# Square sums of attention heads' outputs: squares as float32 weights against one column of ones

## The chip, the cores and the metric

The kernel runs on one core of one Trainium2 chip, as one launch. The metric is device time in microseconds (us) of that core. Three runs of the kernel before took 1516.12, 1515.57 and 1514.3 us; their median is 1515.57 us.

## The reference, cut to what matters

One encoder layer: RMSNorm, a combined projection, a pooling branch and a differential-attention branch, gates, an output projection, and an MLP. The part that the change touches is the normalisation of each head's output in the attention branch:

```python
def head_rmsnorm(x, g):
    xf = x.astype(jnp.float32)
    return xf * lax.rsqrt(jnp.mean(xf * xf, axis=-1, keepdims=True) + EPS) * g.astype(jnp.float32)

    o = o.transpose(1, 0, 2, 3, 4).reshape(B, S, N_HEADS, V_HEAD_DIM)
    o = head_rmsnorm(o, g_sub) * (1.0 - lambda_init)
```

There are 8 heads, 1024 positions, and 128 values a head and position (`V_HEAD_DIM`). For each head and position the sum of 128 squares is needed.

## The kernel before, in words

All large products run on TensorE in "fp32r" pieces: an operand is split in a high and a low part (`split`, L135 on ACT makes the high part, L136 on DVE or POOL the low one), and `mm3` (L142 to L144) makes three matmuls of them. The kernel has an attention stage, a stage that combines the branches, and the MLP. The attention stage works in groups, one for each pair of head h and block t of 128 positions (64 groups). In each group one token of every kind of work is set down, each for a group some places back: A the projection z for a block (`stage_qkv`), B and C the norms and transposes of q and k, D the scores and softmax (`stage_scores`, L783 to L803), E the transposes of the attention weights (`stage_aT`, L839), F the product with V (`stage_pv`), H the square sums (`stage_ssq`), R the finished norm of a whole head (`stage_norm`, L886). F and H run for every second block, so for 4 pairs p of blocks in each of 8 heads: 32 times each. Beside these, "fillers" set down the projections of the gates (tiles g) and of the pooling branch (tiles u, yp), one unit every second group. A scheduler then sets the order of the instructions on each engine from the kernel's data dependencies, this order of tokens and its own estimate of the times. Each engine runs its list strictly in that order.

What happens to one pair of blocks: `stage_pv` accumulates the head's output, transposed (128 values by 256 positions), in columns 0 to 255 of the PSUM tile `po`. ACT squares it into the SBUF tile `oq` (L863), copies it to `oS` (L864), and the copy goes to DRAM (L865). Then `split` (L869) makes the tile `oqs` of the squares' high part (ACT, L135) and low part (DVE, L136). In `stage_ssq` a 128 by 128 matrix of ones is the weight operand, and the high and low parts stream past it (L876, L877, 256 columns each): columns 256 to 511 of `po` get the sums over the 128 partitions, the same in every row. DVE multiplies each 128 by 128 half with the identity and adds up along the rows (L879, a multiply-and-reduce, followed by a read of its accumulator), so that position q's sum lands in row q of one column of `SS`. Once a head has all 8 columns of `SS`, `stage_norm` works out the factor r (L890 to L895), transposes it on TensorE (L897, tile `trr`), copies it to `rT` on ACT (L899) and stores it (L900); `y_pair` loads it back for the output of the heads (tiles yr, yb, later `by`).

The tile `po` has a single buffer, and so have `oq` and `oqs`. The matrix `ones` is of type fp32r; `f(ones)` reads the same bytes as float32. A matmul whose operands are float32 or fp32r loads its own weights: a trace shows the load as a row of the engine PEld and the product as a row of PE. The transposes (L739, L839, L897) are matmuls in transpose mode, with the float32 data as weights and the identity `identf` streaming past.

Of the kernel before, what the change touches and what calls it, by code (L numbers as in the profile page):

```python
# [9 lines left out]
F32R = mybir.dt.float32r  # L10
I32 = mybir.dt.int32
AF = mybir.ActivationFunctionType
ALU = mybir.AluOpType
# [4 lines left out]
P = 128  # L18
# [49 lines left out]
def encoder_kernel(  # L68
# [21 lines left out]
    nc = tc.nc  # L90
    x, out = x[0], out[0]
# [20 lines left out]
    def pad(pool_, n):  # L112
        pool_.tile([P, n], F32, tag=f"pad{n}", name=f"pad{n}")
# [16 lines left out]
    def f(ap):  # L130
        return ap.bitcast(F32)

    def split(hi, lo, src, lo_eng=None):

        made = nc.scalar.copy(hi, src)  # L135
        (lo_eng or nc.vector).tensor_tensor(lo, src, f(hi), op=ALU.subtract)  # L136
        return made

    def mm3(ps, lhs_hi, lhs_lo, rhs_hi, rhs_lo, first, last, more=False):

        kw = {"skip_group_check": True} if more else {}
        nc.tensor.matmul(ps, lhs_hi, rhs_hi, start=first, stop=False, **kw)  # L142
        nc.tensor.matmul(ps, lhs_hi, rhs_lo, start=False, stop=False, **kw)  # L143
        return nc.tensor.matmul(ps, lhs_lo, rhs_hi, start=False, stop=last, **kw)  # L144
# [62 lines left out]
    identf = const.tile([P, P], F32, name="identf")  # L207
    make_identity(nc, identf)
    ones = const.tile([P, P], F32R, name="ones")
# [211 lines left out]
    with ExitStack() as ph:  # L421
# [5 lines left out]
        def s1(shape, dt, name, tag, bufs=1):  # L427
            return sp.tile(shape, dt, tag=tag, name=name, bufs=bufs)
# [249 lines left out]
        st = {}  # L678
        ATs = {}
        Zs = {}  # L680
        SS = {}
# [167 lines left out]
        def stage_pv(h, p):  # L849
            V, views = KV[h][1], ATs.pop((h, p))[0]  # L850
            po = ps_o.tile([P, 512], F32, tag="o", name=f"po{h}_{p}")
            nkt = 2 * p + 2
            for kt in range(nkt):
                v = V[kt // 4]
                mm3(
                    po[:, 0:256], v[:, kt % 4, 0, :], v[:, kt % 4, 1, :],
                    views[kt][0], views[kt][1], kt == 0, kt == nkt - 1,
                )
                if kt % 2 and kt < nkt - 1:
                    yield  # L860
            oS = s1([P, 256], F32, f"oS{h}_{p}", "oS", 2)
            oq = s1([P, 256], F32, f"oq{h}_{p}", "oq")
            nc.scalar.activation(oq, po[:, 0:256], AF.Square)  # L863
            nc.scalar.copy(oS, po[:, 0:256])  # L864
            nc.scalar.dma_start(y_dram[h * P : (h + 1) * P, p * 256 : (p + 1) * 256], oS)  # L865
            if not (h or p):
                pad(sp, 16)
            oqs = s1([P, 2, 256], F32R, f"oqs{h}_{p}", "oqs")
            split(oqs[:, 0, :], oqs[:, 1, :], oq)  # L869
            st[h, p, "o"] = (po, oq, oqs)  # L870
            yield

        def stage_ssq(h, p):

            po, oq, oqs = st.pop((h, p, "o"))
            nc.tensor.matmul(po[:, 256:512], ones, oqs[:, 0, :], start=True, stop=False)  # L876
            nc.tensor.matmul(po[:, 256:512], ones, oqs[:, 1, :], start=False, stop=True)  # L877
            for i in range(2):
                nc.vector.tensor_tensor_reduce(  # L879
                    out=oq[:, i * P : (i + 1) * P], in0=po[:, 256 + i * P : 256 + (i + 1) * P], in1=identf,  # L880
                    scale=1.0, scalar=0.0, op0=ALU.mult, op1=ALU.add,
                    accum_out=SS[h][:, 2 * p + i : 2 * p + i + 1],
                )
            yield

        def stage_norm(h):  # L886
# [21 lines left out]
        def stage(w, g):  # L908
            h, t = divmod(g, NT)
            if w == "A":  # L910
                if t == 0:
                    head_start(h)
                yield from stage_qkv(h, t)
            elif w == "B":
                yield from stage_prep(h, t)
            elif w == "C" and t % 2:
                yield from stage_qkT(h, t - 1)
            elif w == "D":
                yield from stage_scores(h, t)
            elif w == "E":  # L920
                yield from stage_aT(h, t)
            elif w == "F" and t % 2:
                yield from stage_pv(h, t // 2)
            elif w == "H" and t % 2:
                yield from stage_ssq(h, t // 2)
            elif w == "R" and t == NT - 1:
                yield from stage_norm(h)
            elif w == "W" and t == 0 and h:
                for kp in range(NK // 2):
                    load_w(h, kp)  # L930
                    split_w(h, kp, nc.gpsimd)
# [61 lines left out]
        for g in range(-2, N + 10):  # L993
# [33 lines left out]
            for tok in ORDER:  # L1027
                if tok not in gens:
                    i = g - tok[1]
# [767 lines left out]
```

## Time and profile before

| | |
|---|---|
| median of three runs | 1515.57 us |
| the profiled execution's own time | 1515.89 us |
| its span, first to last instruction | 1514.1 us |
| PE (matmuls) busy | 1506.0 us, 7590 instructions |
| PEld (weight loads) busy | 1308.1 us, 7590 instructions |
| DVE busy | 1062.3 us |
| ACT busy | 809.3 us |
| POOL busy | 352.5 us |
| granted TensorE clock | 1.00 throughout |

The profile is of one execution. PE's rows show when a matmul starts and a modelled end: successive matmuls overlap, so the busy time of a row is longer than what it adds. What a matmul adds to PE's time is read from the distance between one start and the next. In a timeline the columns are the start, the duration, the engine, the line and operation, the tiles (written<-read), the shapes and a count; in square brackets stands how long the engine sat idle before it, and what ended that.

### The profile page before, as it was taken

The numbers are of one execution on the slowest core, as the hardware profiler recorded it, in microseconds if no ns is written. First come the engines' busy times: TensorE is split into PE (matmuls) and PEld (weight loads), VectorE is DVE, ScalarE is ACT, GpSimd is POOL, SyncE is SP. The second block draws the span as 40 slices with busy tenths as digits, with TensorE's granted clock in tenths as the row PEclk, the third lists the DMA queues.
The fourth block names the chain that finished last, engine by engine and source line by source line (L and its number), as shares of the span: only waits on it lengthen the run. The fifth ranks groups of instructions, "written<-read, shape, count | busy, mean of one in ns | idle before, by whom it ended". The sixth has DMA issues, their size and how long they took to land.

```text
span 1514.1 us, 22055 instructions
## 1 busy us (share of the span) xinstructions
PE 1506.0 (99%) x7590; PEld 1308.1 (86%) x7590; DVE 1062.3 (70%) x2170; ACT 809.3 (53%) x1671; POOL 352.5 (23%) x457
## 2 busy tenths in 40 slices
PE   9999999999999999999999999999999999999999
PEld 8999998999999989888888888888888888888887
DVE  7776768877888777745469899667656687556662
ACT  6656566655656564653544477556555634333331
POOL 4545644353526453321330000000000000000000
PEclk9999999999999999999999999999999999999999
DMA  7223333422434344437865734454433799437750
GB/s 228 70 85 118 105 97 108 126 87 65 150 117 147 98 129 151 160 117 248 308 216 195 237 132 144 156 187 154 152 125 112 285 361 388 161 125 259 227 189 28
DMA packets 211210, 247.86 MB, mean 164 GB/s; under 512 B 12981, under 2 KB 146074, under 8 KB 211098
## 3 DMA queue, kind: packets, MB, share of 16 engines
q1 hardware_dynamic: 193530, 219.01, 43.7%
q10 hardware_dynamic: 17568, 27.44, 4.9%
q8 instruction: 60, 0.98, 0.3%
q14 instruction: 52, 0.43, 0.1%
HBM read 172.97 MB, written 73.43 MB: 163 GB/s over the span
## 4 chain that ended last, share of the span: by engine, by line
PE 96%; DMA 1%; ACT 1%; DVE 1%; issue 1%; SPq 0%; POOL 0%; DVEq 0%; ACTq 0%; POOLq 0%
PE z L144 5%; PE z L142 5%; PE z L143 5%; PE Da L143 4%; PE Da L142 4%; PE Da L144 4%; PE g L142 4%; PE g L144 4%; PE g L143 4%; PE X L142 3%; PE X L144 3%; PE Db L143 3%; PE Db L142 3%; PE X L143 3%; PE Db L144 3%; PE sc L783 2%
## 5 line engine op out<-in xcount | busy, mean ns | idle before, releaser
L144 PE MATMUL z<-wqkv,hT 128*128 128x384 f32 x512 | 174.0, 340 | 0.0
L142 PE MATMUL z<-wqkv,hT 128*128 128x384 f32 x512 | 173.5, 340 | 0.3 <-ACT hT L445 0.2
L143 PE MATMUL z<-wqkv,hT 128*128 128x384 f32 x512 | 172.9, 338 | 0.0
L794 ACT ACTIVATE s<-s,nm 128x256 f32<-128x256 f32 (+7 forms) x128 | 99.4, 777 | 77.6 <-DVE nm L786 76.8
L716 POOL TENSOR_TENSOR ms<-ms,mhalf 128x4 f32<-128x4 f32 x64 | 71.1, 1110 | 164.4 <-DVE ms L715 162.9
L142 PE MATMUL g<-hT,fwgate 128*128 128x512 f32 x256 | 101.2, 395 | 0.6 <-ACT yps L340 0.4
L144 PE MATMUL g<-hT,fwgate 128*128 128x512 f32 x256 | 100.8, 394 | 0.0
L143 PE MATMUL g<-hT,fwgate 128*128 128x512 f32 x256 | 100.6, 393 | 0.0
L142 PEld LDWEIGHTS z<-wqkv,hT 128*128 128x128 f32 x512 | 96.3, 188 | 3.2 <-ACT hT L445 0.8
L143 PEld LDWEIGHTS z<-wqkv,hT 128*128 128x128 f32 x512 | 96.3, 188 | 2.5 <-DVE wqkv L445 0.3
L144 PEld LDWEIGHTS z<-wqkv,hT 128*128 128x128 f32 x512 | 96.2, 188 | 2.3 <-DVE hT L445 0.5
L786 DVE CUSTOM_DVE_ANT_0 s<-sc,dist 128x512 f32<-128x512 f32 (+3 forms) x128 | 71.8, 567 | 19.4 <-PE sc L784 13.8
L136 DVE TENSOR_TENSOR AS<-s,AS 128x512 fp32r<-128x512 f32 x64 | 43.4, 686 | 33.9 <-ACT AS L135 33.8
L783 PE MATMUL sc<-K,Q 128*128 128x512 f32 (+2 forms) x192 | 66.5, 351 | 0.2 <-DVE nm L786 0.2
L784 PE MATMUL sc<-K,Q 128*128 128x512 f32 (+2 forms) x192 | 65.0, 345 | 0.0
L136 POOL TENSOR_TENSOR wqkv<-rqkv,wqkv 128x384 fp32r<-128x384 f32 x56 | 58.9, 1069 | 23.2 <-ACT wqkv L135 22.9
L136 POOL TENSOR_TENSOR fwgate<-frgate,fwgate 128x512 fp32r<-128x512 f32 x32 | 43.7, 1367 | 58.4 <-ACT fwgate L135 58.3
L142 PEld LDWEIGHTS g<-hT,fwgate 128*128 128x128 f32 x256 | 48.1, 188 | 9.4 <-ACT yps L340 0.7
L144 PEld LDWEIGHTS g<-hT,fwgate 128*128 128x128 f32 x256 | 48.1, 188 | 9.2
L143 PEld LDWEIGHTS g<-hT,fwgate 128*128 128x128 f32 x256 | 48.1, 188 | 8.6
L136 DVE TENSOR_TENSOR AT_0l<-ta,AT_0h 128x512 fp32r<-128x512 f32 (+1 forms) x48 | 31.9, 666 | 30.1 <-ACT AT_0h L135 26.2
L379 POOL TENSOR_TENSOR wd<-wd 128x128 f32<-128x128 f32 (+1 forms) x64 | 50.2, 791 | 8.6 <-ACT wd L981 5.9
(513 smaller groups left out, 4614.6 us busy)
## 6 DMA issues: line engine op xcount, KB each, us to landing
wd<-in_w_down_dram SPq DMA_DIRECT2D x48, 512.0 KB, 5.4
wu<-in_w_up_dram SPq DMA_DIRECT2D x32, 512.0 KB, 4.4
udS<-us SPq DMA_DIRECT2D x64, 256.0 KB, 3.7
ur<-udS SPq DMA_DIRECT2D x32, 512.0 KB, 3.5
rqkv<-in_w_in_dram SPq DMA_DIRECT2D x64, 192.0 KB, 2.8
ur<-ud SPq DMA_DIRECT2D x24, 512.0 KB, 4.5
frgate<-in_w_gate_dram SPq DMA_DIRECT2D x32, 256.0 KB, 2.6
g_dram<-go ACTq DMA_DIRECT2D x32, 256.0 KB, 2.0
```

The lines of the kernel that those rows point to most:

```text
L136: (lo_eng or nc.vector).tensor_tensor(lo, src, f(hi), op=ALU.subtract)
L142: nc.tensor.matmul(ps, lhs_hi, rhs_hi, start=first, stop=False, **kw)
L143: nc.tensor.matmul(ps, lhs_hi, rhs_lo, start=False, stop=False, **kw)
L144: return nc.tensor.matmul(ps, lhs_lo, rhs_hi, start=False, stop=last, **kw)
L379: eng.tensor_tensor(out_, a, b, op=ALU.subtract)
L716: powered[0] = nc.gpsimd.tensor_tensor(ms, ms, mhalf[:, 0:4], op=ALU.pow)
L783: nc.tensor.matmul(dst, Q[:, i, 0, :], rhs, start=True, stop=False)
L784: nc.tensor.matmul(dst, Q[:, i, 1, :], rhs, start=False, stop=True)
L786: nc.vector.tensor_tensor_reduce(out=s[i][:, c : c + w], in0=sc[:, 0:w], in1=dist[:, o0 + c : o0 + c + w], scale=2.0 ** -(h + 1), scalar=B ...
L794: exped[0] = nc.scalar.activation(s[i][:, 0:n], s[i][:, 0:n], AF.Exp, bias=last, scale=-1.0, accum_out=Z[:, i, t : t + 1])
```

## The change

The squares are no longer split in two parts, and the tile `oqs` is gone. In `stage_ssq` the roles are turned: a 128 by 128 half of `oq`, read as float32, is the weight operand, and one column of the ones, read as float32, streams past it. The result is one column of `po` with position q's sum in row q. There are two such matmuls, one for each half, in place of the two fp32r matmuls of 256 columns. ACT copies the two columns to `SS`; the identity, the multiply-and-reduce and the accumulator reads on DVE are gone. The rest of the kernel's text is the same.

```diff
-            oqs = s1([P, 2, 256], F32R, f"oqs{h}_{p}", "oqs")
-            split(oqs[:, 0, :], oqs[:, 1, :], oq)
-            st[h, p, "o"] = (po, oq, oqs)
+            st[h, p, "o"] = (po, oq)
             yield
 
         def stage_ssq(h, p):
 
-            po, oq, oqs = st.pop((h, p, "o"))
-            nc.tensor.matmul(po[:, 256:512], ones, oqs[:, 0, :], start=True, stop=False)
-            nc.tensor.matmul(po[:, 256:512], ones, oqs[:, 1, :], start=False, stop=True)
+            po, oq = st.pop((h, p, "o"))
             for i in range(2):
-                nc.vector.tensor_tensor_reduce(
-                    out=oq[:, i * P : (i + 1) * P], in0=po[:, 256 + i * P : 256 + (i + 1) * P], in1=identf,
-                    scale=1.0, scalar=0.0, op0=ALU.mult, op1=ALU.add,
-                    accum_out=SS[h][:, 2 * p + i : 2 * p + i + 1],
-                )
+                nc.tensor.matmul(po[:, 256 + i : 257 + i], oq[:, i * P : (i + 1) * P], f(ones)[:, 0:1], start=True, stop=True)
+            nc.scalar.copy(SS[h][:, 2 * p : 2 * p + 2], po[:, 256:258])
             yield
```

In the changed kernel the two matmuls are line 875 and the copy is line 876. The scheduler makes the lists anew, so other instructions change places too. Here are two places around the first pair of blocks of the seventh head (h = 6, p = 0). On PE, before; `po_0` is the pair's PSUM tile, z and g are projections, sc scores, trr the transposed factor of the head before:

```order
L142 MATMUL z_0_6889<-wqkv_5_6661,hT_0_0_186 128x384
L897 MATMUL trr_6751<-identf,r_6744 8x128
L876 MATMUL po_0_6766<-oqs_0_6778,ones 128x256
L877 MATMUL po_0_6766<-oqs_0_6778,ones 128x256
L143 MATMUL z_0_6889<-wqkv_5_6661,hT_0_0_186 128x384
L144 MATMUL z_0_6889<-wqkv_5_6661,hT_0_1_187 128x384
L142 MATMUL z_0_6889<-wqkv_6_6667,hT_0_0_188 128x384
L142 MATMUL g_1_6822<-hT_1_0_461,fwgate_0_6571 128x512
```

On PE, in the changed kernel:

```order
L142 MATMUL z_0_6789<-wqkv_2_6553,hT_0_0_184 128x384
L783 MATMUL sc_4_0_0_6771<-K_0_5853,Q_4_6627 128x384
L875 MATMUL po_0_6670<-ones,oq_0_6678 128x1 x2
L784 MATMUL sc_4_0_0_6771<-K_0_5853,Q_4_6627 128x384
L143 MATMUL z_0_6789<-wqkv_2_6553,hT_0_0_184 128x384
L144 MATMUL z_0_6789<-wqkv_2_6553,hT_0_1_185 128x384
L142 MATMUL z_0_6789<-wqkv_3_6556,hT_0_0_184 128x384
L890 MATMUL trr_6655<-identf,r_6648 8x128
```

The two matmuls of a pair stand side by side, and earlier: two of the projection z's eight steps are done there, where five were.

On ACT at the same place, before; K, Q and V are the head's operands, s its scores, wqkv the next head's weights:

```order
L864 COPY oS_0_6773<-po_0_6766 128x256
L135 CAST wqkv_5_6661<-rqkv_2_6655 128x384
L712 ACTIVATE sq<-z_7_6781 128x4x64
L135 CAST V_1_5940<-z_7_6781 128x128
L755 CAST Q_4_6723<-tk_4_6718 64x256
L750 ACTIVATE K_1_5938<-tk_4_6718,ggh_5943 64x256
L135 CAST oqs_0_6778<-oq_0_6774 128x256
L865 DMA y_dram<-oS_0_6773 128x256
L135 CAST wqkv_6_6667<-rqkv_3_6664 128x384
```

On ACT, in the changed kernel, from the last instructions ahead of the new copy:

```order
L752 CAST Q_4_6627<-tk_4_6622 64x256
L135 CAST wqkv_5_6565<-rqkv_2_6559 128x384
L876 COPY SS_5858<-po_0_6670 128x2
L341 DMA p_dram<-yps_1_6720 128x512
L135 CAST wqkv_6_6571<-rqkv_3_6568 128x384
L892 COPY rT_6657<-trr_6655 8x128
L135 CAST wqkv_7_6574<-rqkv_3_6568 128x384
L893 DMA r_dram<-rT_6657 8x128
L755 CAST Q_4_6627<-tk_4_6622 64x256
```

The cast of the squares is gone from the list, and the copy of the sums stands eleven places behind the copy to `oS`; casts of the next head's weights stand behind it.

## Prediction

> **What bounds the kernel now.** I read the page's busy times first, then busy times by stretch, then PE's timeline.
>
> ```profile
> span 1514.1 us, 22055 instructions
> ...
> PE 1506.0 (99%) x7590; PEld 1308.1 (86%) x7590; DVE 1062.3 (70%) x2170; ACT 809.3 (53%) x1671; POOL 352.5 (23%) x457
> ```
>
> PE is busy for 1506.0 of 1514.1 us. The instructions in question run between 70 and 690 us (their rows are below), in the attention stage, so I ask for the busy times of that stretch and of the rest:
>
> ```profile
> 70.00:690.00 620.00, 617.92 (x3560) 567.71 (x3559) 460.26 (x1276) 363.89 (x899) 279.66 (x359) 1.00 0.37 118
> 690.00:1514.00 824.00, 819.84 (x3648) 678.60 (x3646) 551.17 (x757) 398.39 (x651) 41.40 (x34) 1.00 0.58 199
> ```
>
> The columns after the length are PE, PEld, DVE, ACT and POOL, then the granted clock. In the stage PE idles 2.1 of 620 us, at full clock; DVE is free for 160 us and ACT for 256 us. Behind it PE idles 4.2 of 824 us. So a step that PE does more or less moves the end by nearly its own length, and a step of DVE or ACT counts only where PE stands still for it.
>
> PE's rows overlap, so what a matmul adds is read from start to start. This is PE's timeline at one of the 32 places (start, duration, line):
>
> ```profile
> 306.10 0.34 PE L784 MATMUL sc<-K,Q 128*128 128x384 f32 x1
> 306.27 0.28 PE L876 MATMUL po<-oqs,ones 128*128 128x256 f32 x1
> 306.39 0.27 PE L897 MATMUL trr<-identf,r 128*8 128x128 f32 x1
> 306.41 0.42 PE L142 MATMUL z<-wqkv,hT 128*128 128x384 f32 x1
> 306.67 0.28 PE L877 MATMUL po<-oqs,ones 128*128 128x256 f32 x1
> 306.79 0.34 PE L143 MATMUL z<-wqkv,hT 128*128 128x384 f32 x1
> ...
> 307.38 0.34 PE L142 MATMUL z<-wqkv,hT 128*128 128x384 f32 x1
> 307.55 0.49 PE L839 MATMUL ta<-identf,s 128*128 128x128 f32 x3
> 307.80 0.42 PE L143 MATMUL z<-wqkv,hT 128*128 128x384 f32 x1
> 308.06 0.34 PE L144 MATMUL z<-wqkv,hT 128*128 128x384 f32 x1
> 308.23 0.34 PE L142 MATMUL z<-wqkv,hT 128*128 128x384 f32 x1
> ```
>
> Two prices come out. A matmul of the old pair takes 0.12 us of PE (306.27 to 306.39, 306.67 to 306.79), a matmul of 384 columns 0.17 (307.38 to 307.55). The three transposes have float32 weights of 128 by 128: from 307.55 to 308.06 three of them and one z pass, 0.51 us; less 0.17 for the z, 0.34 remain, 0.11 each. They stream 128 columns, half of what the old pair's matmuls do, yet cost nearly as much. So I read 0.11 as the time of a weight load that no long stream covers. The transpose of r shows the same from the other side: it streams 128 columns too, but loads only 8 columns of weights, and the next matmul starts 0.02 us after it.
>
> **The change part by part.** *PE.* Removed: 2 fp32r matmuls in each of 32 places, 2 x 0.12 = 0.24 us a place, 7.7 us in all. Added: 2 matmuls a place with float32 weights of 128 by 128 and a stream of one column. The stream is next to nothing, so the price is that of the loads, and the question is how many there are. The trace of before has no plain float32 matmul. The changed program as built answers it: its list for TensorE holds 7654 weight loads and 7654 matmuls, where the page counts 7590 of each before. 7590 less the 64 removed plus 64 x 2 is 7654: each new matmul is executed as two loads, each with a pass of its own. A place then has four loads instead of two, 4 x 0.11 = 0.44 us by the transposes' price, or 0.20 more than before; 32 x 0.20 = 6.4 us more on PE.
>
> The bounds of that price: below, the two loads of a matmul cost together what a transpose's one does, 2 x 0.11 = 0.22 a place, 0.02 less than before, a gain of 0.6 us. Above, each load also carries two passes of its stream (high and low part of the ones), and each further pass costs a start-to-start of the kind seen at 306.39 (0.02, call it 0.03): 4 x 0.14 = 0.56, 0.32 more, 10.2 us. The rows of the loads themselves (time of all, then mean ns of one) lead to the same upper end:
>
> ```profile
> L143 PEld LDWEIGHTS z<-wqkv,hT 128*128 128x128 f32 x512 | 96.3, 188 | 2.5 <-DVE wqkv L445 0.3
> ...
> L839 PEld LDWEIGHTS ta<-identf,s 128*128 128x128 f32 x288 | 35.7, 140 | 6.5 <-DVE AT L136 1.0 <-ACT V L135 0.8
> ```
>
> Neither is what a load adds, since loads overlap their neighbours: the transposes come 0.11 apart with loads of 0.140. If the new loads did not overlap at all, four of 0.140 would again be 0.56. I take 0.11 a load, since the transposes are the only float32 weights in the trace that stand side by side under short streams, as the new ones do.
>
> The Trainium skill, FP8 and Floating Point Precision, TensorE Precision Notes, says that a true FP32 product takes four passes through the array (high and low part of each operand), and TensorE: Matmul & The Clock Gate, Terms, says that the transpose mode is four times faster for FP32, so that a transpose's price would not be a plain float32 matmul's. No run shown here has a plain float32 matmul; if each of four passes cost a load, the sum would be the last rival's below.
>
> *DVE.* Removed, from the views of the two tiles and of line 879:
>
> ```profile
> L135 ACT CAST oqs<-oq x32: 391/407/425, 75.2 to 680.1; 128x256 fp32r<-128x256 f32 x32
> L136 DVE TENSOR_TENSOR oqs<-oq,oqs x32: 404/426/1231, 76.3 to 680.5; 128x256 fp32r<-128x256 f32 x32
> ```
>
> ```profile
> L879 DVE CUSTOM_DVE_ANT_0 oq<-po,identf x64: 238/285/292, 78.4 to 685.5; 128x128 f32<-128x128 f32 x64
> L879 DVE DVE_READ_ACCUMULATOR2_ANT SS<- x64: 75/83/86, 78.7 to 685.7; 128x1 f32 x64
> its engine sat idle before it (us, times) until:
>   PE po L877: 3.9, 6
> ```
>
> By the medians (ns), 32 x 426 + 64 x 285 + 64 x 83 = 37.2 us of DVE go. It is off PE's path but for the places where PE waits for DVE, and those are few:
>
> ```profile
> 249.62 0.39 PE L142 MATMUL yp<-mix,wgrp 128*128 128x512 f32 x1
> 249.85 0.40 PE L143 MATMUL yp<-mix,wgrp 128*128 128x512 f32 x1
> 250.09 0.40 PE L144 MATMUL yp<-mix,wgrp 128*128 128x512 f32 x1
> 250.86 0.63 PE L839 MATMUL ta<-identf,s 128*128 128x128 f32 x4 [0.38 <-DVE s L803]
> 252.30 0.44 PE L839 MATMUL ta<-identf,s 128*128 128x128 f32 x2 [0.81 <-DVE AT L136]
> 252.90 0.51 PE L783 MATMUL sc<-K,Q 128*128 128x512 f32 x1 [0.17 <-DVE nm L786]
> ```
>
> ```profile
> 542.55 0.36 PE L876 MATMUL po<-oqs,ones 128*128 128x256 f32 x1
> 543.08 0.38 PE L877 MATMUL po<-oqs,ones 128*128 128x256 f32 x1 [0.16 <-DVE oqs L136]
> ...
> 543.64 0.34 PE L142 MATMUL z<-wqkv,hT 128*128 128x384 f32 x1
> 544.37 0.50 PE L142 MATMUL g<-hT,fwgate 128*128 128x512 f32 x1 [0.39 <-ACT yps L340]
> ```
>
> Start to start less the usual price (0.23 for 512 columns, 0.11 a transpose, 0.12, 0.17): 0.54, 1.00, 0.38, 0.41 and 0.56, together 2.9 us. That is all that a lighter DVE and ACT can return here. One of them, the 0.41 at L877, waits for the removed split itself and goes for certain; the others depend on where the new lists put things. I take nothing for them and keep 2.9 us as the lower end.
>
> *ACT.* The cast (407 ns, above) goes, a copy of 128 by 2 comes; the nearest row is the copy of the 8 by 128 factor:
>
> ```profile
> L899 ACT COPY rT<-trr x8: 238/256/257, 152.0 to 694.0; 8x128 f32<-8x128 f32 x8
> ```
>
> ACT wins some 0.15 us a place, 4.8 us in all, under 256 us of free time. But the copy must wait for PE's pair, where the cast waited for ACT's own square. Behind it on ACT stand the casts of the next head's weights and of Q, for which PE waits later. Before, DVE waited for L877 6 times, 3.9 us in all; if ACT waits as long and PE feels half, that is 2 us, and nothing if the list has the copy late, as at the place shown (eleven places behind the copy to oS). Value taken: nothing; upper end 2 us.
>
> *The tail.* The last head's sums feed r, r_dram, the tiles yr and then by, whose products start only here:
>
> ```profile
> L142 PE MATMUL bX<-by,wa x16: 389/389/389, 740.3 to 750.5; 128*128 128x512 f32 x16
> ...
> L135 ACT CAST by<-ry x15: 615/619/624, 706.8 to 751.9; 128x512 fp32r<-128x512 f32 x15
> ```
>
> The first cast ends 33 us ahead of the first product, so the copy's 0.26 us in this chain costs nothing. No DMA is added or moved past another queue by the code itself.
>
> *Sum.* +6.4 us on PE, nothing elsewhere: 1515.89 + 6.4 = 1522.3 for the profiled execution, whose own time lies 0.3 us above the median of the three runs; against the median, 1515.57 + 6.4 = 1522.0. The case's own range: all 2.9 us of waits returned, 1519.1; 0.14 a load, 1525.8.
>
> **The rivals.** (1) *One load's price.* The two loads of a matmul overlap, or the second is so short that a matmul costs 0.11 in all. For it: the only float32 weights in the trace do cost 0.11. Against: they are counted once each, the new ones twice. Result: 0.6 us less, up to 2 us of waits less: 1513 to 1515, no change that can be told (3 us, 0.2%, is about what a measurement of this kernel tells from none).
>
> (2) *Faster, the waits go.* The mechanism is DVE's queue: 37.2 us less in it, and PE finds s, AT and nm ready at 250 and 543 us. With all of the 2.9 us returned, the sum changes its sign where a load adds 0.083 us: 32 x (4 x 0.083 - 0.24) = 2.9. A gain over 3 us needs 0.059 and less, which is the price of (1): 1515.57 - 0.6 - 2.9 = 1512.1. For it: PE's waits in the stage are mostly for DVE. Against: the 0.11, and that the last of the five waits is for ACT.
>
> (3) *The new order stalls.* The lists are made anew on every engine; a wait of PE such as that at 252.30 (1.0 us) may come up at two to five new places, with ACT's copy in front of the casts as the likeliest. 1522.0 + 2 to 5: 1524 to 1527. For it: PE has no slack. Against: DVE and ACT both have less to do.
>
> (4) *Every pass loads.* Four passes a matmul, each at 0.11: 8 x 0.11 = 0.88 a place, 0.64 more, 20.5 us: 1536.1. Against: the built program has two loads a matmul. By the four passes of the Trainium skill's page this is the time, if none of them is hidden.
>
> **How the numbers follow.** The forecast 0.75, (1) 0.12, (2) 0.04, (3) 0.05, (4) 0.04. The likeliest gives 1522.0. The forecast's own 1519.1 to 1525.8 and (3) are in the range; I widen it to 1517 below, for a load slightly under 0.11 with some waits returned, and to 1528 above, for a load of 0.14 together with ACT's 2 us (1527.8). Left out are (1), (2) and (4), 0.20. Slower by over 0.2% are the forecast, (3) and (4), 0.84; within 0.2% is (1), 0.12; faster is (2), 0.04.
>
> **What would show it.** Right: PE and PEld count 7654, line 875 appears 128 times on each; from the start of the first of a group to the next z after it about 0.44 us more than the z alone; DVE's busy time near 1025 us, ACT's near 804.5; idle PE in the attention stage near 2 us; the stage from 70 us to the last L875 about 6 us longer, the rest unchanged. Wrong: starts of line 875 0.05 us apart (1), 64 rows in place of 128, or 0.2 apart (4), or waits on ACT's copy (3).

## The result, and the profile after

The changed kernel takes 1519.37 us (median of 11 runs, 1518.5 to 1519.9), the kernel before 1515.54 us beside it (11 runs, 1514.3 to 1516.12): a ratio of 1.0025, 95% interval 1.0016 to 1.0034. It is 3.8 us slower. Forecast were 6.4 us, 1522.0, in a range from 1517 to 1528. The profiled executions differ by 3.3 us (1515.89 and 1519.16; spans 1514.1 and 1517.3).

The page of the changed kernel, its busy times:

```profile
span 1517.3 us, 22020 instructions
...
PE 1511.0 (100%) x7654; PEld 1314.8 (87%) x7654; DVE 1026.0 (68%) x2010; ACT 801.2 (53%) x1671; POOL 355.0 (23%) x457
```

PE and PEld count 7654, as the built program did; DVE lost 36.3 us, ACT 8.1. Now the busy times of the attention stage (PE, PEld, DVE, ACT, POOL):

```profile
70.00:690.00 620.00, 619.63 (x3611) 571.40 (x3610) 423.68 (x1114) 354.93 (x898) 282.44 (x358) 1.00 0.37 117
```

PE idles 0.4 us of 620 where it idled 2.1. The instructions of the new line on PE, and the copy on ACT, by their lines:

```profile
L875 PEld LDWEIGHTS po<-ones,oq x128: 187/192/225, 77.2 to 686.8; 128*128 128x128 f32 x128
L875 PE MATMUL po<-ones,oq x128: 164/250/250, 77.4 to 686.8; 128*128 128x1 f32 x128
...
  ACT SS L876: 2.3, 4
```

```profile
L876 ACT COPY SS<-po x32: 137/160/172, 78.8 to 687.1; 128x2 f32<-128x2 f32 x32
```

Each of the 64 matmuls is two loads and two passes: 128 rows of each. ACT waited for them 4 times, 2.3 us in all, and its copy took 0.16 us, not the 0.26 of the nearest row. PE's timeline at one of the 32 places shows the price:

```profile
213.77 0.34 PE L143 MATMUL z<-wqkv,hT 128*128 128x384 f32 x1
213.94 0.50 PE L875 MATMUL po<-ones,oq 128*128 128x1 f32 x4
214.31 0.42 PE L144 MATMUL z<-wqkv,hT 128*128 128x384 f32 x1
214.56 0.33 PE L142 MATMUL z<-wqkv,hT 128*128 128x384 f32 x1
```

From 213.94 to 214.56 stand four passes and one z: 0.62 us, less 0.17 for the z, 0.45, or 0.112 a load. Here and below, "a load" in such a price means one weight load with its one short pass: every run here has them in equal number, so only the two together have a price. Over the 32 places that is 32 x (0.45 - 0.24) = 6.7 us more than the old pairs.

What brings 6.7 down to 3.8 is in the same timeline, near the place where PE had waited for s, AT and nm:

```profile
250.05 0.34 PE L144 MATMUL z<-wqkv,hT 128*128 128x384 f32 x1
250.23 0.60 PE L839 MATMUL ta<-identf,s 128*128 128x128 f32 x4
250.58 0.42 PE L142 MATMUL z<-wqkv,hT 128*128 128x384 f32 x1
...
251.37 0.34 PE L143 MATMUL z<-wqkv,hT 128*128 128x384 f32 x1
251.54 0.38 PE L839 MATMUL ta<-identf,s 128*128 128x128 f32 x2
251.68 0.42 PE L144 MATMUL z<-wqkv,hT 128*128 128x384 f32 x1
```

The four and the two transposes stand there without a gap, and z matmuls lie between them. The one longer wait left in the stage is a new one, of 0.5 us:

```profile
383.34 0.33 PE L142 MATMUL z<-wqkv,hT 128*128 128x384 f32 x1
384.04 0.45 PE L143 MATMUL z<-wqkv,hT 128*128 128x384 f32 x1 [0.37 <-POOL wqkv L136]
```

### The profile page after: what moved, and what is told of

It is laid out like the page before. It is cut to its first block, busy times and chain, and to the rows that moved or that the text cites. A ratio compares the mean times of both kernels' runs of the same rounds, so it can differ in the third digit from the quotient of the medians.

```text
span 1517.3 us, 22020 instructions
## 1 busy us (share of the span) xinstructions
PE 1511.0 (100%) x7654; PEld 1314.8 (87%) x7654; DVE 1026.0 (68%) x2010; ACT 801.2 (53%) x1671; POOL 355.0 (23%) x457
## 4 chain that ended last, share of the span: by engine, by line
PE 99%; DVE 1%; ACT 0%; issue 0%; POOL 0%; DVEq 0%; ACTq 0%; POOLq 0%
PE z L144 6%; PE z L143 6%; PE z L142 6%; PE g L143 4%; PE g L144 4%; PE g L142 4%; PE Da L144 4%; PE Da L143 4%; PE Da L142 4%; PE X L142 3%; PE Db L144 3%; PE X L144 3%; PE Db L143 3%; PE X L143 3%; PE Db L142 3%; PE sc L783 2%
```

## The experiments

Theory: the time is the sum of two terms, PE's loads (+6.7 us; the expectations write 6.6) and waits of PE that go because DVE has 37 us less to do. First rival: the waits went because the scheduler made new lists that happened to fall well. Second rival: float32 matmuls of one column have another price than their loads. The first four runs take the change apart.

**TensorE's part as before, DVE's part gone** (against the kernel before):

```diff
-            oq = s1([P, 256], F32, f"oq{h}_{p}", "oq")
+            oq = s1([P, 256], F32R, f"oq{h}_{p}", "oq")
...
-            oqs = s1([P, 2, 256], F32R, f"oqs{h}_{p}", "oqs")
-            split(oqs[:, 0, :], oqs[:, 1, :], oq)
...
-            nc.tensor.matmul(po[:, 256:512], ones, oqs[:, 0, :], start=True, stop=False)
-            nc.tensor.matmul(po[:, 256:512], ones, oqs[:, 1, :], start=False, stop=True)
-            for i in range(2):
-                nc.vector.tensor_tensor_reduce(
...
+            nc.tensor.matmul(po[:, 256:512], ones, oq, start=True, stop=False)
+            nc.tensor.matmul(po[:, 256:512], ones, oq, start=False, stop=True)
+            nc.scalar.copy(SS[h][:, 2 * p : 2 * p + 2], po[:, 256:258])
```

> TensorE's part as before, DVE's part gone: ACT writes the squares as fp32r, both old 256-column matmuls read that one tile, and ACT copies two columns of their result. The low parts and the diagonal are left out, so the sums are not the reference's. Theory (the sum is PE's loads plus PE's waits for DVE that go): PE's work is that of before, and the 2.6 us of waits over 0.15 us that the trace of before has and that of the changed kernel has not are returned by the lighter DVE: 1515.5 - 2.6 = 1512.9 us, 1512 to 1514. Rival (the waits went because the lists were made anew and fell well, not because of DVE's load): a new list falls as it may, 1515.5 and up to 2 us either way, with waits of PE for DVE in the attention stage as before.

Measured: 1514.19 us, ratio 0.9991 (0.9982 to 1.0): 1.3 us less, half of what the theory had, and just outside its range; the interval ends at 1, so the gain is only just told from none. ACT's cast of the squares is gone here too, and its copy is there, as in the changed kernel. The busy times of the stage and the longest of PE's waits in it:

```profile
70.00:690.00 620.00, 618.54 (x3568) 568.73 (x3567) 429.96 (x1116) 355.88 (x900) 281.92 (x359) 1.00 0.37 117
```

```profile
408.48 0.34 PE L143 MATMUL z<-wqkv,hT 128*128 128x384 f32 x1
409.79 0.44 PE L839 MATMUL ta<-identf,s 128*128 128x128 f32 x2 [0.97 <-DVE AT L136]
```

The waits of before are gone, but PE still idles 1.5 us, at a place where it had not waited: DVE's lighter queue is not enough by itself; the list of instructions seems to have a say.

**TensorE's part as changed, DVE's part kept** (against the changed kernel):

```diff
+            oqs = s1([P, 2, 256], F32R, f"oqs{h}_{p}", "oqs")
+            split(oqs[:, 0, :], oqs[:, 1, :], oq)
...
+            idle = s1([P, 2], F32, f"idle{h}_{p}", "idle")
+            for i in range(2):
+                nc.vector.tensor_tensor_reduce(
+                    out=f(oqs[:, i, 0:P]), in0=po[:, 130:258], in1=identf,
+                    scale=1.0, scalar=0.0, op0=ALU.mult, op1=ALU.add,
+                    accum_out=idle[:, i : i + 1],
+                )
```

> TensorE's part as changed, DVE's part kept: the split of the squares on ACT and DVE and the two multiply-and-reduce passes of DVE behind the matmuls stay, their results unused. Theory: the loads cost 32 x (4 x 0.112 - 0.24) = 6.6 us and DVE's waits are back: 1515.5 + 6.6 = 1522.1 us, 1521 to 1523. Rival (the lists): as the changed kernel, 1519.4 us, since DVE's 37 us are under cover.

Measured: 1521.62 us, ratio 1.0041 (1.0028 to 1.0053), as the theory had it: 2.2 us over the changed kernel. With DVE's work back, PE idles 1.4 us in the stage:

```profile
70.00:690.00 620.00, 618.57 (x3600) 569.78 (x3599) 455.29 (x1267) 364.07 (x927) 278.11 (x357) 1.00 0.37 116
```

But the two longest waits in the stage name ACT, not DVE:

```profile
150.07 0.27 PE L899 MATMUL trr<-identf,r 128*8 128x128 f32 x1
150.90 0.50 PE L142 MATMUL g<-hT,fwgate 128*128 128x512 f32 x1 [0.56 <-ACT go L349]
...
628.54 0.49 PE L839 MATMUL ta<-identf,s 128*128 128x128 f32 x3
629.49 0.66 PE L839 MATMUL ta<-identf,s 128*128 128x128 f32 x4 [0.46 <-ACT Q L755]
```

This kernel also has the cast of the squares back on ACT, beside the new copy. So the time fits the theory, but that DVE's queue made these waits is not shown: the cast on ACT or the new list may have.

**One load a matmul** (against the changed kernel):

```diff
-            oq = s1([P, 256], F32, f"oq{h}_{p}", "oq")
+            oq = s1([P, 256], F32R, f"oq{h}_{p}", "oq")
...
-                nc.tensor.matmul(po[:, 256 + i : 257 + i], oq[:, i * P : (i + 1) * P], f(ones)[:, 0:1], start=True, stop=True)
-            nc.scalar.copy(SS[h][:, 2 * p : 2 * p + 2], po[:, 256:258])
+                nc.tensor.matmul(po[:, 256 + 2 * i : 258 + 2 * i], oq[:, i * P : (i + 1) * P], ones[:, 0:2], start=True, stop=True)
+            nc.scalar.copy(SS[h][:, 2 * p : 2 * p + 2], po[:, 256:260:2])
```

> As changed, but ACT rounds the squares to fp32r as it writes them, and they are fp32r weights against two columns of the ones: the low parts of the squares are left out. The built list has 7590 loads, so one load a matmul. Theory (the price is 0.112 us a load): 2 x 0.112 - 0.24 = -0.02 us a place, -0.5 us, and the waits go as in the changed kernel: 1515.5 - 0.5 - 2.6 = 1512.4 us, 1511.5 to 1513.5. Rival (float32 or one-column matmuls have a price of their own beside the load): 0.15 us or more a matmul, 1514 us or more.

Measured: 1512.90 us, ratio 0.9983 (0.9975 to 0.9992). It is faster than both kernels, 6.5 us under the changed one for 64 loads fewer, 0.10 us each. The trace has 64 rows of each kind, and at one place:

```profile
147.24 0.28 PE L875 MATMUL po<-ones,oq 128*128 128x2 f32 x2
147.38 0.43 PE L143 MATMUL z<-wqkv,hT 128*128 128x384 f32 x1
147.64 0.33 PE L144 MATMUL z<-wqkv,hT 128*128 128x384 f32 x1
```

Two passes and a z take 0.40 us, less 0.17, 0.115 a load. The second rival falls: a load with a short pass costs the same in fp32r and in float32, and a plain float32 matmul costs two of them and nothing beside.

**Every float32 matmul twice** (against the changed kernel):

```diff
                 nc.tensor.matmul(po[:, 256 + i : 257 + i], oq[:, i * P : (i + 1) * P], f(ones)[:, 0:1], start=True, stop=True)
+                nc.tensor.matmul(po[:, 258 + i : 259 + i], oq[:, i * P : (i + 1) * P], f(ones)[:, 0:1], start=True, stop=True)
```

> As changed, but each of the two float32 matmuls is made twice, the second time into two columns that nobody reads. Theory: four more loads a place, 32 x 4 x 0.112 = 14.3 us: 1519.4 + 14.3 = 1533.7 us, 1532.5 to 1535. Rival (the four loads run partly under waits of PE that are there anyway): under 1531 us.

Measured: 1532.99 us, ratio 1.0115 (1.0102 to 1.0129): 13.6 us for 128 more loads, 0.106 each. That is 0.7 us less than the theory's 14.3, so at most a twentieth of it was hidden.

The next two runs give the same work other lists, by setting the square sums down one group later:

```diff
-O = "B1 C2 H7 D4 R8 E5 F6 W-2 A0"
+O = "B1 C2 H8 D4 R8 E5 F6 W-2 A0"
```

**The kernel before with H8.**

> The kernel before with its square sums set down one group later (token H8 instead of H7), so the same work in other lists. Theory (the waits follow DVE's load): waits of PE over 0.15 us in the attention stage stay at 2 to 3.5 us, as in the two kernels run so far with DVE's part in place (3.1 and 2.3), and the time at 1515 to 1516.5 us. Rival (the luck of the lists): waits under 1 us and 1513 to 1514 us are as likely.

Measured: 1516.97 us beside 1515.83 for the kernel before, ratio 1.0008 (0.9999 to 1.0017). It came out 0.5 us above the theory's range; no change can be told. PE idles 1.7 us in the stage:

```profile
70.00:690.00 620.00, 618.29 (x3557) 567.16 (x3556) 457.23 (x1274) 365.31 (x899) 278.85 (x359) 1.00 0.37 117
```

**The changed kernel with H8.**

> The changed kernel with token H8 instead of H7. Theory: DVE's load is as light as in the changed kernel, so waits over 0.15 us in the attention stage are 0.5 to 1.8 us, as in the four kernels run so far without DVE's part (0.5 to 1.8), and the time is 1519 to 1521 us. Rival (lists): waits of 2 to 3 us, 1521 to 1522.5 us.

Measured: 1521.79 us, ratio 1.0042 (1.0029 to 1.0054), 2.4 us above the changed kernel and in the rival's range. DVE has no more to do than in the changed kernel, yet PE idles 2.0 us in the stage, and one wait is as long as the worst of before:

```profile
70.00:690.00 620.00, 618.05 (x3597) 569.14 (x3596) 428.39 (x1113) 354.08 (x896) 280.94 (x359) 1.00 0.37 115
```

```profile
412.72 0.33 PE L143 MATMUL z<-wqkv,hT 128*128 128x384 f32 x1
414.19 0.44 PE L839 MATMUL ta<-identf,s 128*128 128x128 f32 x2 [1.13 <-DVE AT L136]
```

So the list alone moves these kernels by up to 2.4 us, as much as the waits in question.

**128 columns of ones instead of one** (against the changed kernel):

```diff
-                nc.tensor.matmul(po[:, 256 + i : 257 + i], oq[:, i * P : (i + 1) * P], f(ones)[:, 0:1], start=True, stop=True)
-            nc.scalar.copy(SS[h][:, 2 * p : 2 * p + 2], po[:, 256:258])
+                nc.tensor.matmul(po[:, 256 + i * P : 256 + (i + 1) * P], oq[:, i * P : (i + 1) * P], f(ones), start=True, stop=True)
+            nc.scalar.copy(SS[h][:, 2 * p : 2 * p + 2], po[:, 256:512:P])
```

> The changed kernel with all 128 columns of the ones streaming past each float32 weight half, instead of one; ACT copies every 128th column. Theory (the load is the price, and a stream up to its length hides under it): a stream of 128 fp32r columns lies under 0.11 us here, and if float32 streams take twice the passes they just fill it: starts 0.11 to 0.12 apart, 1519 to 1521 us. Rival (each pass of a float32 stream adds its own time, another 0.05 us a pass at 128 columns, two a load): 0.16 to 0.21 apart, 32 x 4 x 0.05 to 0.1 = 6 to 13 us more, 1526 to 1532 us.

Measured: 1520.38 us, ratio 1.0031 (1.0019 to 1.0043), 1.0 us above the changed kernel: 128 times the columns for nearly the same time.

```profile
147.43 0.34 PE L142 MATMUL z<-wqkv,hT 128*128 128x384 f32 x1
147.61 0.61 PE L875 MATMUL po<-ones,oq 128*128 128x128 f32 x4
147.97 0.42 PE L783 MATMUL sc<-K,Q 128*128 128x384 f32 x1
148.23 0.34 PE L143 MATMUL z<-wqkv,hT 128*128 128x384 f32 x1
```

From 147.61 to 148.23 again 0.62 us for four passes and a 384-column matmul. The price of a load with its pass stays the same up to 128 columns, so below that it is not the stream that sets it. That it is the load is argued from this, not shown.

Three more runs repeat the first three with H8, to see which term holds in two sets of lists.

**TensorE's part as before, DVE's part gone, H8.**

> TensorE's part as before and DVE's part gone (as in the first experiment, low parts and diagonal left out), with token H8. Theory (three terms that add: loads, DVE's part 1.4 to 2.3 us, the list with H8 1.3 to 2.4 us more): 1517.0 less 1.4 to 2.3: 1514.7 to 1515.6 us. Rival (DVE's part did nothing, the lists did it all): as the kernel before with H8, 1516.5 us or more.

Measured: 1514.41 us, ratio 0.9991 (0.9982 to 1.0); 2.6 us under the kernel before with H8, 0.3 below the theory's range.

**TensorE's part as changed, DVE's part kept, H8.**

> TensorE's part as changed and DVE's part kept (results unused), with token H8. Theory: the changed kernel with H8, 1521.8 us, plus DVE's 1.4 to 2.3: 1523.2 to 1524.1 us. Rival: as the changed kernel with H8, 1521.3 to 1522.3 us.

Measured: 1524.11 us, ratio 1.0051 (1.0038 to 1.0064), at the theory's upper end; but the profile, whose execution took the same 1524.11 us, shows that the time came from elsewhere. In the stage PE idles only 0.2 us. Behind it, it waits for ACT's evacuation of a gate tile (go), and this is what follows:

```profile
706.54 0.39 PE L144 MATMUL bp<-ypT,wbp 128*128 128x512 f32 x1
708.76 0.50 PE L142 MATMUL bp<-ypT,wbp 128*128 128x512 f32 x1 [1.83 <-ACT go L349]
709.10 0.39 PE L143 MATMUL bp<-ypT,wbp 128*128 128x512 f32 x1
...
710.03 0.59 PE L144 MATMUL bp<-ypT,wbp 128*128 128x512 f32 x1
710.42 0.63 PE L142 MATMUL bp<-ypT,wbp 128*128 128x512 f32 x1
...
713.41 0.43 PE L143 MATMUL bp<-ypT,wbp 128*128 128x512 f32 x1
```

On ACT two casts of by stand ahead of that evacuation and wait 8.3 us for a DMA:

```profile
706.99 1.14 ACT L135 CAST by<-ry 128x512 fp32r<-128x512 f32 x2 [8.31 <-DMA ry<-ys]
708.03 0.68 ACT L349 ACTIVATE go<-g,cols 128x512 f32<-128x512 f32 x1
```

The wait costs 2.0 us (2.22 from start to start, less 0.23), and the eight matmuls from 710.03 to 713.41 take 0.42 us each instead of 0.23, 1.5 us more. Without these 3.5 us this execution would be under the changed kernel with H8. The five executions also fall in two groups: three took 1524.1 to 1524.7 us at a mean granted clock of 0.999, two took 1522.1 and 1522.7 us at 1.000, which is what one would see if the slow stretch came in three of them; only one was profiled. So the agreement with the expected number is luck and proves nothing here.

**One load a matmul, H8.**

> One fp32r load a matmul (low parts of the squares left out), with token H8. Theory: 7.1 us of loads (64 of 0.112) under the changed kernel with H8: 1521.8 - 7.1 = 1514.7 us, 1513.7 to 1515.7. Rival (the lists matter more than the loads): 1512.9 us as with H7, or over 1516.

Measured: 1513.68 us, ratio 0.9988 (0.9978 to 0.9997), just at the theory's lower end: 8.1 us under the changed kernel with H8, and 0.8 us above the same kernel with H7.

The runs together, medians in us (the kernel before took 1515.54, 1515.83 and 1515.80 in the three sittings, so differences between sittings are good to some 0.3):

| | H7 | H8 |
|---|---|---|
| TensorE as before, DVE's part kept (the kernel before) | 1515.5 | 1517.0 |
| TensorE as before, DVE's part gone | 1514.2 | 1514.4 |
| two loads a matmul, DVE's part kept | 1521.6 | 1524.1 |
| two loads a matmul, DVE's part gone (the changed kernel) | 1519.4 | 1521.8 |
| one load a matmul, DVE's part gone | 1512.9 | 1513.7 |

TensorE's part costs 6.1, 5.2, 7.1 and 7.4 us, 6.4 on average: the first term stands. DVE's part (with the cast on ACT, which comes and goes with it) costs 1.3, 2.2, 2.6 and 2.3, all of one sign, though the last of them mostly by the wait behind the stage and what followed it. The list with H8 costs 1.4, 0.2, 2.5, 2.4 and 0.8. So the second term is about as large as what a new list does, and neither the theory nor the first rival can be ruled out for it. How much of the changed kernel's returned waits is owed to DVE's lighter queue, how much to ACT's lighter one, and how much to where its list happens to stand, stays open: only the range of 1.3 to 2.6 us for all together is shown.

The change itself costs 3.8 us with H7 and 4.8 with H8 (1521.79 less 1516.97), in both less than its loads.

## Why the prediction was right, point by point

**What bounds the kernel: right.** Every load that was added or taken away moved the end by 0.10 to 0.13 us. Of DVE's 36 us little came back.

**Two loads a matmul at 0.11: right.** The trace has 128 rows of line 875 and 0.112 us a load; the forecast term of 6.4 us measures 6.7 in the trace and 5.2 to 7.4 in four comparisons. The transposes were the right row to take. The two ends of its range are excluded: one load's price by the 128 rows and their starts, 0.14 a load by 0.106 in the doubled run. The longer row of a load (192 ns against a transpose's 140) meant nothing for what it adds.

One reading on the way was wrong. The next matmul does start 0.02 us behind the transpose of r, but that z then holds PE for 0.26 us (306.41 to 306.67) instead of 0.17, so the transpose of r costs 0.11 too, though it loads 8 columns of weights and not 128. It is no sign that the 0.11 is the time of the load, and the 0.02 is not the price of a further pass, from which the upper end was taken. The forecast rests on neither.

The page cited for the transposes' price differs: the Trainium skill, TensorE: Matmul & The Clock Gate, Terms, has the transpose mode four times faster for FP32; with 128 columns streaming, as in a transpose, the plain product took two passes 0.11 apart where a transpose takes one, so twice the time. The four passes of the Trainium skill, FP8 and Floating Point Precision, TensorE Precision Notes, would fit two loads with two passes each; the trace has one row of PE for each load, so no run here shows them one by one.

**Nothing for DVE's and ACT's waits: the step that was mis-sized.** The prediction listed five waits of PE, 2.9 us, and took nothing for them, "the others depend on where the new lists put things". In the changed kernel none of the five is left and one new wait of 0.5 us stands: 2.4 us returned. 6.7 - 2.4 = 4.3 us, against 3.3 in the profiled executions and 3.8 in the medians. Part of the rest is a sixth wait of before, which the list left out; it is for ACT:

```profile
624.72 0.92 PE L839 MATMUL ta<-identf,s 128*128 128x128 f32 x7
625.82 0.50 PE L142 MATMUL g<-hT,fwgate 128*128 128x512 f32 x1 [0.17 <-ACT go L349]
626.16 0.39 PE L143 MATMUL g<-hT,fwgate 128*128 128x512 f32 x1
```

From 624.72 to 626.16 are 1.44 us, less 7 x 0.11 and 0.23, 0.44. It is gone too, which leaves 3.9 us; what still differs is no more than the rounding of the price makes (0.005 us a load is 0.6 over 128 loads). So "all that a lighter DVE and ACT can return" was short by 0.4 us. The lower end of the case's own range, all waits returned, 1519.1, is where the time came out, since the sixth wait and the new one nearly cancel. That so much came back with this very list was in part luck: with H8 the changed kernel idles 2.0 us in the stage again and takes 1521.79 us, near the 1522.0 that was forecast, while the kernel before takes 1516.97. To take nothing was too cautious in both lists; the reason, a lighter queue or the list, stays open, as said above.

**ACT: right in sign.** It lost 8.1 us, not 4.8, since the copy is shorter than the row taken for it. The copy made it wait 2.3 us in all (the upper end took 3.9), and PE's waits show none for it. **The tail: right.** The chain kept its cover; in the changed kernel the first cast of by and the first product that uses it start at:

```profile
L142 PE MATMUL bX<-by,wa x23: 389/389/389, 743.6 to 769.4; 128*128 128x512 f32 x23
...
L135 ACT CAST by<-ry x19: 603/618/624, 708.4 to 767.5; 128x512 fp32r<-128x512 f32 x19
```

**The rivals.** (1) and (2) needed a cheaper load and fell with it, though the waits of (2) did go. (3) named the right mechanism, new lists with new waits, for the wrong kernel: it shows with H8 (2.4 us), not in the changed kernel. (4) needed four loads a matmul. Of the signs named, three were wrong: idle PE in the stage near 2 us (0.4), ACT near 804.5 us (801.2), and the stage 6 us longer. The last of L875 starts at 686.8 us, 1.9 behind the last matmul of the old pair:

```profile
L877 PE MATMUL po<-oqs,ones x32: 277/280/384, 78.1 to 684.9; 128*128 128x256 f32 x32
```

The first bX moved by 3.3 us, the loads less the waits.

## What to carry to other kernels

Where PE has no slack, a weight load with a short stream cost 0.11 us here, whatever it computed (fp32r, float32 or a transpose, 1 to 128 columns): count the loads, and count a plain float32 matmul twice. Turning a wide stream into a narrow one gains nothing if it turns one covered load into several that stand side by side; with one load each the same idea was the fastest version here (the squares rounded to fp32r, their low parts left out, 1512.9 us). And when work leaves the queues that PE's few waits name, add those waits to the sum at some value, with an error as large as a new list makes (here up to 2.4 us).

## What the runs showed of the hardware that was not expected

In one profile a wait of PE came with a loss of about twice its length. In the run with DVE's part kept and H8, 1.83 us of idle were followed, 1.3 us after PE had resumed, by about 3.4 us at half the clock. The busy times by stretch (the last three numbers are the granted clock, the DMA's share and GB/s):

```profile
709.00:710.00 1.00, 1.00 (x5) 0.81 (x5) 0.75 (x2) 0.74 (x2) 0.00 (x0) 1.00 0.83 286
710.00:713.00 3.00, 3.00 (x9) 2.30 (x8) 2.67 (x5) 1.66 (x3) 0.44 (x1) 0.51 0.97 343
```

The wait of 1.13 us in the changed kernel with H8 had no such sequel: the clock stayed at 1.00.

The Trainium skill, TensorE: Matmul & The Clock Gate, Part 1, has the clock fall to half after an idle window of about 3.4 us, free-running, and rise again after a busy one: the length of the slow stretch agrees, but the idle time ahead of it was 1.83 us here. That the wait caused the slow stretch is argued from their order in one execution, not shown.
